# Hybrid mixer: decay rows through DRAM, fewer products for dt and group sums, three modulation blocks moved, taps and roots ordered ahead of splits

## Chip, core and metric

The kernel runs on one core of a Trainium2 chip. The metric is the device time of one execution in microseconds. The kernel before took 1097.56 us, the median of three runs (1096.56 to 1098.46).

## What is computed

The reference runs one sequence of 256 tokens with 1024 channels through two layers of three sublayers each: a feed-forward block (FFN), a mixer, and a second FFN. The mixer of the first layer is the hybrid that this change is about, that of the second layer is an mLSTM. A condition vector `c` modulates each sublayer: a product with `ada_w` gives nine blocks of shifts, scales and gates in a layer. The hybrid's core:

```python
gate_lru, x_lru, z_ssd, xbc, dt_raw = jnp.split(h @ w_in, HYB_SPLITS, axis=-1)
x_lru = causal_conv(x_lru, lru_conv_w, lru_conv_b)
y_lru = rg_lru(x_lru, ...) * jax.nn.gelu(gate_lru.astype(f32))
xbc = jax.nn.silu(causal_conv(xbc, ssd_conv_w, ssd_conv_b)).astype(f32)
dt = jax.nn.softplus(dt_raw.astype(f32) + ssd_dt_bias.astype(f32))
a = -jnp.exp(ssd_a_log.astype(f32))
y = ssd_chunked(xs, dt, a, bm, cm) + ssd_d.astype(f32)[:, None] * xs
y = y.reshape(bsz, seq, SSD_WIDTH) * jax.nn.silu(z_ssd.astype(f32))
y = rms_norm(y.reshape(bsz, seq, SSD_GROUPS, SSD_WIDTH // SSD_GROUPS), ...)
y_cat = jnp.concatenate([y_lru, y], axis=-1).astype(h.dtype)
return y_cat @ w_out
```

`ssd_chunked` cuts the tokens into two chunks of 128. For each of 16 heads it needs the running sum `acs` of `dt * a` in a chunk, and from it `decay_in = exp(acs[t] - acs[s])` for all pairs t >= s of a chunk and `decay_out = exp(acs[t])`.

## The kernel before

**Layout and stages.** Activations lie transposed: channels on the 128 partitions, the 256 tokens along the free dimension, so `x` is eight tiles of [128, 256]. All large weights lie in one stream of 128x128 tiles, in the order of use, loaded in pieces of eight tiles (512 KB) by the SP queue. The program is unrolled; six sublayers (0 to 5) follow one another. Sublayer 0 (first FFN) uses pieces 0 to 65, sublayer 1 (hybrid) pieces 66 to 119.

**Products.** Precision comes from splitting: a weight piece is cast to a high part by ScalarE (`whi`, L101) and its rest is computed by VectorE (`wlo`, L102). `multiply` (L436) issues three products for each tile: high times high, high times low, low times high. They are counted in `W.products`, three for each tile, 24 for each piece; "product n of stage s" below is that count. `h[k]` holds the high and low part of the modulated input beside each other.

**Order of work.** `Weights.next` (L123) hands out tiles; it loads and splits up to four pieces ahead (`LEAD`) into four raw buffers and six high and six low buffers. Splits are in order on each engine. `W.behind(piece, n, ins)` puts the ScalarE (n = 0) or VectorE (n = 1) half of a piece's split behind an instruction in that engine's order. `pump(i)` issues the modulation blocks that `ADA_PLAN` makes due at piece i: a DMA of 512 KB on the SP queue and one product with accumulation on VectorE (`ada`, L262), behind the last split so far. The compiler's scheduler orders the rest by its own estimate of times; every engine and the SP queue then run in that fixed order. `stand(ins, s, n)` (L312) keeps an instruction behind product n - 1 of stage s; `in_one_go` keeps a group of products together in order.

**The hybrid (L769).** `begin` computes the four B and C channels first, with the norm's sum (`rst_n1`) and spread (`rsb_n1`) put between the products. Then:
- Two and then six `xbc` channels are projected; each is convolved by one ScalarE step and three VectorE taps (`conv`, L728). They take turns in the four PSUM banks of tag `mm`, so a later projection waits for an earlier one's last tap.
- dt (L815 to L826): eight input tiles times a 128-column window whose first 16 columns are the dt weights, with three products for each tile (24 in all), copied out, transposed, and turned into dt by VectorE.
- The loop over c from 0 to 9 (L934) projects `xl` c, and from c = 2 on `z` c - 2 and the gates of the LRU. At c = 3 `decay_sums` makes `acs`. At c = 4 `decay_rows` transposes it to 16 rows and writes a high part and a rest into `stk` (rows 0 to 15 and 32 to 47).
- The loop over pairs of heads m0 = 0, 2, 4, 6 (L967): four `ab` products of a selecting column (`sel`) with `stk` put the rows of four heads on all partitions in PSUM; ScalarE makes `mt` (eight Relus with the bias `acs`, one Exp) and `ce` (two Exps), VectorE multiplies them with `cbt` and C; then 12 products give `y`. After that `xs` is updated and squared into `gacc`, and two `gl` channels (the LRU's gate) are projected.
- After m0 = 2 and m0 = 6 the group's sum `rst_g` is taken: four products over the two halves of `gacc`, which the profile shows as eight passes. Nine small VectorE steps make the reciprocal root (`rs_tokens`, `rsqrt_small`), two products spread it (`rsb_g`), and `group_norm` applies it.
- The output projection (`out_project`, L535) runs over `ys` of group 0, `ys` of group 1, and then `yl`, and traces the LRU's scans (L1057), the second `group_norm` and the gelu beside its products. It starts at product 912 of the stage; the part on group 1 starts at 1008, that on `yl` at 1104.

`mt` tiles and the `xw` tiles of `ssd_values` share two buffers (tag `mt`).

## Time and profile before

| | |
|---|---|
| median of three runs | 1097.56 us (1096.56 to 1098.46) |
| the profiled execution | 1097.25 us |
| its span, first to last instruction | 1095.5 us |
| TensorE busy | 1083.8 us, 99% |
| VectorE busy | 920.5 us, 84% |
| ScalarE busy | 639.5 us, 58% |
| mean granted TensorE clock | 0.999 |

The profile is of one execution. The page gives sums and groups; the timeline lists instructions in order of time for one engine (PE is TensorE, DVE VectorE, ACT ScalarE, SP the queue that issues DMAs), with the idle time ahead of one in brackets and what ended it. A matmul's duration there overlaps that of the next, so the time that a product costs is read from the distance of starts. Tile names stand without their numbers: `wlo` is the low part of any piece. The hybrid stage lies at about 194 to 367 us of the span.

### The profile page before, as it was taken

The page shows a single profiled execution, that of the slowest core. Times are in us where ns is not written, and L with a number is a line of the kernel's source. Part 1 is how long each engine was busy: PE and PEld are TensorE (multiplying, and loading weights), DVE is VectorE, ACT ScalarE, POOL GpSimd, SP SyncE. Part 2 cuts the span into 40 slices and gives each one's busy share as a digit, 9 for nine tenths or more (in the row PEclk, how much of TensorE's full clock was granted, in tenths as well). Part 3 has the DMA queues.
Part 4 walks back from the last instruction along what each step waited for, and adds up shares of the span by engine and source line. Part 5 has one row for each costly group of instructions (what it writes and reads, how often), then busy time and mean ns, then how long its engine had stood idle before and what let it go on. Part 6 is the DMA issues. An engine that isn't in the chain of part 4 may idle for free.

```text
span 1095.5 us, 23272 instructions
## 1 busy us (share of the span) xinstructions
PE 1083.8 (99%) x9315; PEld 1070.4 (98%) x9315; DVE 920.5 (84%) x1654; ACT 639.5 (58%) x1053; POOL 8.8 (1%) x28
## 2 busy tenths in 40 slices
PE   9999999999999999999999999999999999999997
PEld 7999999999999999999999999999999999999997
DVE  7999999899999899989698798979768868866552
ACT  5765555678986564554454455448776655544452
POOL 0000000000000000000000000010000000000000
PEclk9999999999999999999999999999999999999999
DMA  9889999556855489999848799963432664875551
GB/s 375 344 318 391 387 352 343 178 196 195 279 167 191 139 307 370 354 351 327 281 142 323 266 356 346 338 204 119 146 102 81 208 193 137 298 239 193 193 174 39
DMA packets 75534, 272.34 MB, mean 249 GB/s; under 512 B 8593, under 2 KB 9393, under 8 KB 75426
## 3 DMA queue, kind: packets, MB, share of 16 engines
q1 hardware_dynamic: 74592, 269.38, 69.7%
q8 instruction: 73, 1.20, 0.4%
q0 software_dynamic: 400, 1.04, 0.4%
q10 hardware_dynamic: 434, 0.43, 0.1%
q14 instruction: 35, 0.29, 0.1%
HBM read 269.77 MB, written 1.05 MB: 247 GB/s over the span
## 4 chain that ended last, share of the span: by engine, by line
PE 80%; DVE 12%; DMA 4%; issue 2%; ACT 1%; ACTq 0%; DVEq 0%; SPq 0%
PE gu L445 12%; PE gu L444 12%; PE gu L443 11%; PE od L445 10%; PE od L443 10%; PE od L444 10%; DVE wlo L102 4%; DMA wraw<-in_wst_dram 3%; PE zz L445 1%; PE zz L443 1%; PE zz L444 1%; DMA wgr<-in_ml_wg_dram 1%; DVE ada L262 1%; DVE xc L733 1%; PE gu_f L509 1%
## 5 line engine op out<-in xcount | busy, mean ns | idle before, releaser
L102 DVE TENSOR_TENSOR wlo<-wraw,whi 128x1024 fp32r<-128x1024 f32 x364 | 442.9, 1221 | 83.6 <-ACT whi L101 83.0
L101 ACT CAST whi<-wraw 128x1024 fp32r<-128x1024 f32 x364 | 378.2, 1050 | 210.9 <-DMA wraw<-in_wst_dram 80.2
L444 PE MATMUL gu<-hb,whi 128*128 128x256 f32 x1296 | 358.0, 276 | 0.4 <-DVE hb L668 0.3
L443 PE MATMUL gu<-hb,whi 128*128 128x256 f32 x1296 | 358.0, 276 | 0.0
L445 PE MATMUL gu<-hb,wlo 128*128 128x256 f32 x1296 | 357.9, 276 | 0.1
L444 PEld LDWEIGHTS gu<-hb,whi 128*128 128x128 f32 x1296 | 243.3, 188 | 0.8 <-DVE hb L668 0.8
L445 PEld LDWEIGHTS gu<-hb,wlo 128*128 128x128 f32 x1296 | 243.3, 188 | 0.2 <-DVE wlo L102 0.2
L443 PEld LDWEIGHTS gu<-hb,whi 128*128 128x128 f32 x1296 | 243.2, 188 | 0.0
L443 PE MATMUL od<-ph,whi 128*128 128x256 f32 x704 | 194.3, 276 | 0.0
L444 PE MATMUL od<-ph,whi 128*128 128x256 f32 x704 | 194.3, 276 | 0.0
L445 PE MATMUL od<-ph,wlo 128*128 128x256 f32 x704 | 194.3, 276 | 0.0
L262 DVE SCALAR_TENSOR_TENSOR ada<-ada,cact 128x1024 f32<-128x1024 f32 x144 | 175.3, 1218 | 1.4 <-DMA ada<-in_adaT_dram 1.3
L444 PEld LDWEIGHTS od<-ph,whi 128*128 128x128 f32 x704 | 132.1, 188 | 0.0
L445 PEld LDWEIGHTS od<-ph,wlo 128*128 128x128 f32 x704 | 132.1, 188 | 0.0
L443 PEld LDWEIGHTS od<-ph,whi 128*128 128x128 f32 x704 | 132.1, 188 | 0.0
L426 ACT CAST ph<-fg 128x256 fp32r<-128x256 f32 x88 | 35.1, 406 | 114.9 <-DVE fg L595 114.9
L427 DVE TENSOR_TENSOR ph<-fg,ph 128x256 fp32r<-128x256 f32 x88 | 36.4, 421 | 14.2 <-ACT ph L426 14.2
L416 ACT ACTIVATE sq_o<-x 128x256 f32<-128x256 f32 x42 | 17.5, 418 | 45.6 <-DVE x L571 40.6
L571 DVE SCALAR_TENSOR_TENSOR x<-od,gate,x 128x256 f32<-128x256 f32 x48 | 23.1, 481 | 24.4 <-PE od L445 24.2
L444 PE MATMUL zz<-hb,whi 128*128 128x256 f32 x128 | 36.2, 283 | 0.0
L445 PE MATMUL zz<-hb,wlo 128*128 128x256 f32 x128 | 36.1, 282 | 0.0
L443 PE MATMUL zz<-hb,whi 128*128 128x256 f32 x128 | 35.8, 279 | 0.0
(431 smaller groups left out, 1959.1 us busy)
## 6 DMA issues: line engine op xcount, KB each, us to landing
wraw<-in_wst_dram SPq DMA_DIRECT2D x366, 512.0 KB, 4.6
ada<-in_adaT_dram SPq DMA_DIRECT2D x144, 512.0 KB, 5.6
xn<-in_x_dram SPq DMA_DIRECT2D x2, 512.0 KB, 4.0
wgr<-in_ml_wg_dram POOLq DMA_DIRECT2D x3, 256.0 KB, 5.4
out_dram<-res SPq DMA_DIRECT2D x3, 128.0 KB, 2.4
out_dram<-res ACTq DMA_DIRECT2D x1, 256.0 KB
out_dram<-res SPq DMA_DIRECT2D x1, 256.0 KB, 2.9
cols<-in_cols_dram SPq DMA_DIRECT2D x1, 190.0 KB, 9.5
```

The lines of the kernel that those rows point to most:

```text
L101: raw_hi = nc.scalar.copy(hi, raw)
L102: self.last = nc.vector.tensor_tensor(out=lo, in0=raw, in1=hi.bitcast(F32), op=ALU.subtract)
L262: return nc.vector.scalar_tensor_tensor(out=raw, in0=raw, scalar=1.0, in1=cact, op0=ALU.mult, op1=ALU.mult, accum_out=mods[s][:, m:m + 1])
L416: square = nc.scalar.activation(q, x, AF.Square).ins
L426: nc.scalar.copy(hi, src)
L427: nc.vector.tensor_tensor(out=both[:, 1, :], in0=src, in1=hi.bitcast(F32), op=ALU.subtract)
L443: m = nc.tensor.matmul(dst, wh, both[:, 0, :], start=start, stop=False, skip_group_check=True)
L444: W.products += [m, nc.tensor.matmul(dst, wh, both[:, 1, :], start=False, stop=False, skip_group_check=True), nc.tensor.matmul(dst, wl, bo ...
L445: nc.tensor.matmul(dst, wl, both[:, 0, :], start=False, stop=stop, skip_group_check=True)]
L509: W.products += [nc.tensor.matmul(dst, wh, rh, start=(k == 0), stop=False), nc.tensor.matmul(dst, wh, rl, start=False, stop=False), nc.ten ...
L571: nc.vector.scalar_tensor_tensor(out=xs_t[d], in0=dst, scalar=g[:, d:d + 1], in1=xs_t[d], op0=ALU.mult, op1=ALU.add)
L733: nc.vector.scalar_tensor_tensor(out=dst[:, o:], in0=src[:, :T - o], scalar=cw(j), in1=dst[:, o:], op0=ALU.mult, op1=ALU.add)
```

## The change

1. **Decay rows.** `stk`, `sel` and the `ab` products go. ScalarE copies the 16 transposed rows to `rows`; one DMA stores them in a DRAM tile `kept`; for each pair of channel tiles one DMA loads four rows (4 KB) to every partition, straight into `mt`. Exp and Relu then read SBUF. The tiles of m0 = 0 and 2 are loaded at c = 5 and 7 and worked at c = 7 and 9 of the loop (`decay_pair`), those of m0 = 4 and 6 loaded after the squares of m0 = 0 and 2.
2. **dt.** High and low weights lie beside each other in one window, so that two products for each input tile give both sums (16 columns each), and VectorE adds them.
3. **Group sums.** VectorE folds the halves of `gacc` first; the sum takes two products in place of four.
4. **Modulation.** Blocks 40 to 42 move from the hybrid to the first FFN; blocks 16 and 17 come due at pieces 14 and 15 (17 and 18 before), 18 to 42 at pieces 17 to 42, 43 to 47 at pieces 22 to 31 of the hybrid.
5. **Order.** The low splits of four pieces go behind a tap or a root; the first two `y` groups stand at products 732 and 795; the sum of group 1 at 948 and its spread at 976; the sum and spread of `n1` are kept at 11 and 28 from both sides (`hold`); the scans go behind the second root.

```diff
-SUMS = {"n1": (1, 11), "n2": (2, 11), "n4": (4, 14)}
+SUMS = {"n1": (1, 11), "n2": (2, 11), "n4": (4, 14), "g1": (1, 948)}
+KEPT, HELD = ("n1",), 48
+SPREADS = {"n1": (1, 28), "n2": (2, 28), "g1": (1, 976)}
...
-    (0, (17, 43), range(16, 40)), (0, (43, 65), range(48, 64)), (1, (22, 37), range(40, 48)),
+    (0, (14, 16), range(16, 18)), (0, (17, 43), range(18, 43)), (0, (43, 65), range(48, 64)),
+    (1, (22, 34), range(43, 48)),
...
+    dramp = ctx.enter_context(tc.tile_pool(name="dramp", bufs=1, space=bass.MemoryType.DRAM))
...
+    def hold(ins, s, n):
+
+        holds.append((ins, 3 * PIECE * starts[s] + n))
...
+                if i == 0:
+                    W.behind(starts[1] + 9, 1, taps[-1])
...
-            wdh, wdl = (w[:, 16 * k:16 * k + P] for w in dt_parts)
-            nc.tensor.matmul(b[:, 0:T], wdh, h[k][:, 0, :], start=(k == 0), stop=False)
-            nc.tensor.matmul(b[:, 0:T], wdh, h[k][:, 1, :], start=False, stop=False)
-            nc.tensor.matmul(b[:, 0:T], wdl, h[k][:, 0, :], start=False, stop=(k == ND - 1))
+            for i in range(2):
+                nc.tensor.matmul(b[:, 0:T], dt_parts[:, 32 * k:32 * k + P], h[k][:, i, :], start=(k == i == 0),
+                                 stop=(k == ND - 1 and i == 1))
...
+        nc.vector.tensor_tensor(out=dt, in0=both[:, :, 16:32], in1=dt, op=ALU.add)
...
-            nc.vector.tensor_copy(stk[0:16, :], b[0:16, 0:T])
-            nc.vector.tensor_tensor(out=stk[32:48, :], in0=b[0:16, 0:T], in1=stk[0:16, :].bitcast(F32),
-                                    op=ALU.subtract)
+            nc.scalar.copy(rows[0:16, :], b[0:16, 0:T])
+            nc.sync.dma_start(kept, rows[0:16, :])
+
+        def decay_tile(m0):
+            mt = wk.tile([P, 2, 2, 2, P], F32, tag="mt", name=f"mt{m0}", bufs=2)
+            nc.sync.dma_start(mt.rearrange("p n i c t -> p (n i c t)"),
+                                kept.rearrange("(q h) t -> q (h t)", q=4)[m0 // 2:m0 // 2 + 1].to_broadcast([P, 4 * T]))
+            decays[m0] = mt
...
+        def decay_pair(m0):
+            g = m0 // 4
+            mt = decays.pop(m0)
+            ce = wk.tile([P, 2, 2, P], F32, tag="ce", name=f"ce{m0}", bufs=2)
+            expo = nc.scalar.activation(ce.rearrange("p n i t -> p (n i) t"),
+                                        mt.rearrange("p n i c t -> p (n i) c t")[:, :, 1, :], AF.Exp)
...
+                        nc.scalar.activation(mt[:, n, i, c, :], mt[:, n, i, c, :], AF.Relu,
+                                             bias=acs[:, c, hd:hd + 1], scale=-1.0)
+            nc.scalar.activation(mt, mt, AF.Exp, scale=-1.0)
...
+                if c == 7:
+                    W.behind(starts[1] + 31, 1, taps[-1])
...
+            if c in (5, 7):
+                decay_tile(c - 5)
+            if c in (7, 9):
+                pairs[c - 7] = decay_pair(c - 7)
...
-            ab = [ax_bank(f"ab{m}") for m in pair]
-            for m, b in zip(pair, ab):
-                for i in range(2):
-                    hd = 2 * m + i
-                    nc.tensor.matmul(b[:, i * T:(i + 1) * T], sel[:, hd:hd + 1].to_broadcast([P, P]), stk,
-                                     start=True, stop=True)
...
+            mt, ce, needed, expo = pairs.pop(m0) if m0 in pairs else decay_pair(m0)
...
+            if m0 < 4:
+                stand(products[0], 1, (732, 795)[m0 // 2])
...
+                folded = nc.vector.tensor_tensor(out=gacc[:, 0, :], in0=gacc[:, 0, :], in1=gacc[:, 1, :], op=ALU.add)
+            if m0 < 4:
+                decay_tile(m0 + 4)
...
-                roots.append(rs_tokens([gacc[:, 0, :], gacc[:, 1, :]], 512, f"g{g}", "q"))
+                roots.append(rs_tokens([gacc[:, 0, :]], 512, f"g{g}", "q"))
...
+                W.behind(starts[1] + (39, 43)[g], 1, rsqrt_ends[-1])
...
-                nc.vector.tensor_tensor_scan(out=xl[:, c, :], data0=av[:, c, :], data1=nq[:, c, :], initial=0.0,
-                                             op0=ALU.mult, op1=ALU.add)
+                with tc.issue_after(second_root.ins):
+                    nc.vector.tensor_tensor_scan(out=xl[:, c, :], data0=av[:, c, :], data1=nq[:, c, :], initial=0.0,
+                                                 op0=ALU.mult, op1=ALU.add)
...
+    for i, n in holds:
+        for m in W.products[n:n + HELD]:
+            tc.add_manual_dep(m.ins, i.ins.name, NOSYNC, reason="not later")
```

## Rows read from the trace of the kernel before

**Rows 1.** The page: the span, and busy time of the engines.

```profile
span 1095.5 us, 23272 instructions
...
PE 1083.8 (99%) x9315; PEld 1070.4 (98%) x9315; DVE 920.5 (84%) x1654; ACT 639.5 (58%) x1053; POOL 8.8 (1%) x28
```

**Rows 2.** Windows: length; busy PE, PEld, DVE, ACT, POOL; PEclk, DMA, GB/s.

```profile
45.00:60.00 15.00, 15.00 (x135) 15.00 (x134) 12.80 (x18) 12.36 (x23) 0.00 (x0) 1.00 0.73 242
...
60.00:125.00 65.00, 65.00 (x576) 65.00 (x575) 63.37 (x105) 35.77 (x57) 0.00 (x0) 1.00 0.97 367
...
245.00:285.00 40.00, 39.23 (x334) 38.07 (x334) 39.68 (x78) 33.40 (x65) 0.00 (x0) 1.00 0.66 218
```

**Rows 3.** PE timeline (start, us, what), the waits: [idle before <- what ended it].

```profile
220.79 0.36 PE L443 MATMUL xbc<-hb,whi 128*128 128x256 f32 x1 [0.28 <-DVE ssd_x L733]
...
282.85 0.28 PE L445 MATMUL ri<-xlb,wlo 128*128 128x256 f32 x1
...
283.90 0.39 PE L443 MATMUL z<-hb,whi 128*128 128x256 f32 x1 [0.77 <-DVE lru_x L733]
...
296.41 0.33 PE L1008 MATMUL y<-mt,ssd 128*64 128x128 f32 x2 [0.85 <-DVE mt L988]
...
331.61 0.68 PE L405 MATMUL rsb_g<-ident,rsy_g 128*128 128x128 f32 x4 [0.72 <-DVE rsy_g L329]
```

**Rows 4.** Timelines: piece 111's split on DVE, its first use on PE.

```profile
336.61 1.20 DVE L102 TENSOR_TENSOR wlo<-wraw,whi 128x1024 fp32r<-128x1024 f32 x1
...
342.92 0.28 PE L445 MATMUL od<-ysb,wlo 128*128 128x256 f32 x1
```

**Rows 5.** PE timeline: first `dtT` product, and the first after them.

```profile
212.08 0.28 PE L818 MATMUL dtT<-hb,wdh 128*128 128x256 f32 x1
...
214.89 0.28 PE L443 MATMUL xbc<-hb,whi 128*128 128x256 f32 x1
```

**Rows 6.** PE timeline: four `ab` products, a group's sum, and their followers.

```profile
287.45 0.63 PE L974 MATMUL ab<-stk,sel 128*128 128x256 f32 x4
...
287.92 0.28 PE L443 MATMUL gl<-hb,whi 128*128 128x256 f32 x1
...
308.06 1.03 PE L359 MATMUL rst_g<-ones,gacc 128*128 128x1 f32 x8
...
308.95 0.37 PE L444 MATMUL gl<-hb,whi 128*128 128x256 f32 x1
```

**Rows 7.** DVE timeline: a split and an ada product between `xl7`'s taps.

```profile
280.70 1.21 DVE L102 TENSOR_TENSOR wlo<-wraw,whi 128x1024 fp32r<-128x1024 f32 x1
...
282.22 1.22 DVE L262 SCALAR_TENSOR_TENSOR ada<-ada,cact 128x1024 f32<-128x1024 f32 x1
```

**Rows 8.** ACT timeline: `xl7`'s first step, four Relus, an Exp.

```profile
278.08 0.54 ACT L730 ACTIVATE lru_x<-xl,cols 128x256 f32<-128x256 f32 x1
...
292.37 1.18 ACT L983 ACTIVATE mt<-ab,acs 128x128 f32<-128x128 f32 x4
...
293.63 1.14 ACT L986 ACTIVATE mt<-mt 128x1024 f32<-128x1024 f32 x1
```

**Rows 9.** DVE timeline: first and last of the nine steps of `g1`'s root.

```profile
324.43 0.16 DVE L373 TENSOR_SCALAR rsv_g<-rst_g 128x2 f32<-128x2 f32 x1
...
331.33 0.14 DVE L329 SCALAR_TENSOR_TENSOR rsy_g<-rsw_g,rsy_g 128x2 f32<-128x2 f32 x1
```

**Rows 10.** Groups by line, 205 to 345: ada products on DVE.

```profile
L262 DVE SCALAR_TENSOR_TENSOR ada<-ada,cact 128x1024 f32<-128x1024 f32 x8 | 9.7, 1218 | 0.0
```

**Rows 11.** DVE timeline: the first of the two writes of `stk`.

```profile
260.64 0.40 DVE L864 CAST stk<-acst 16x256 fp32r<-16x256 f32 x1
```

**Rows 12.** The page's DMA issues: KB each, median us to landing.

```profile
wraw<-in_wst_dram SPq DMA_DIRECT2D x366, 512.0 KB, 4.6
...
out_dram<-res SPq DMA_DIRECT2D x3, 128.0 KB, 2.4
```

**Rows 13.** SP timeline: two loads of weights, the first to the second's end.

```profile
274.92 2.57 SPq L95 DMA_DIRECT2D wraw<-in_wst_dram  x2
```

More of the change, by code (lines that the diff above doesn't have):

```diff
@@ L364, in sum_tokens @@
                 stand(products[0], *SUMS[nm])
+                if nm in KEPT:
+                    hold(products[-1], *SUMS[nm])
         else:
@@ L406, in spread @@
                                  start=True, stop=True)
-            if nm == "n2" and b == 0:
-                stand(m, 2, 28)
+            if b == 0 and nm in SPREADS:
+                stand(m, *SPREADS[nm])
+            if b == 1 and nm in KEPT:
+                hold(m, *SPREADS[nm])
         return pb[:, 0:T]
@@ L847, in hybrid @@
         acs = acs_wide[:, 0:32].rearrange("p (c h) -> p c h", c=2)
[L848 to L849 removed]
+        rows = sp.tile([P, T], F32, name="rows")
+        kept = dramp.tile([16, T], F32, name="kept")
         dec = sp.tile([P, 16], F32, name="dec")
```

69 lines of the change are left out of this document (33 added, 36 removed).

## The prediction

> **What bounds the kernel now.** I read the page first: TensorE is busy for 1083.8 of 1095.5 us [rows 1], so little time is left in which it waits, and a change pays by taking products off TensorE or by taking away one of its few waits. Whether another engine could hold it back is read from the windows. In the stretch of the hybrid mixer from 245 to 285 us VectorE is busy for 39.68 of 40 us, ScalarE for 33.40, and DMA for 66% [rows 2]: VectorE has no idle time there, and since it works in order, whatever TensorE needs from it waits behind whatever stands ahead of it. The timeline of PE shows four such waits in this stage [rows 3]: `xbc` for a tap, `z` for a tap of `xl7`, `y0` for `mt`, and the spread of `g1` for its root. Each costs a little more than its idle time: between the starts at 282.85 and 283.90 lie 1.05 us instead of one product's 0.12 (below), so the idle 0.77 costs 0.93, 0.16 more. Splits of weights run ahead of TensorE; the smallest lead late in the stage is that of piece 111 (the 110th of the 364 splits), done at 336.61 + 1.20 = 337.81 and first used at 342.92, 5.11 us later [rows 4].
>
> **Products that go.** dt: 24 products of 256 columns take 214.89 - 212.08 = 2.81 us, 0.117 each [rows 5]; 8 go: 0.94 us. Decay rows: four `ab` products take 287.92 - 287.45 = 0.47 us before their follower starts [rows 6]; there are four such fours: 1.88 us. Group sums: the eight passes take 308.95 - 308.06 = 0.89 us [rows 6]; with one operand instead of two half of them go, in two groups: 0.89 us. All of it stands on TensorE, which has nothing else to do in that time: 3.71 us.
>
> **Waits that may go.** With 0.16 added to each idle time of [rows 3], `xbc` costs 0.44, `z` 0.93, `y0` 1.01 and the spread 0.88, together 3.26 us.
> `xbc`: two splits stand ahead of the first taps, and the edit puts the second (piece 75) behind them. It takes a full split, 1.21 us [rows 7], out of the way of a wait of 0.28: I take the wait as gone.
> `z`: a split (280.70) and an ada product (282.22) run between `xl7`'s taps, 1.2 us each [rows 7]. The edit puts the split behind the taps; the ada product may stay. TensorE comes 0.94 + 0.44 = 1.38 us earlier; VectorE is relieved of two `stk` writes before that place, about 0.8. So between nothing and about 0.6 us is left; I take 0.2, since one ada block fewer has run by then.
> `y0`: its pair of decay tiles is made inside the loop, from c = 7, instead of after it. The ACT work of a pair is eight Relus, twice 1.18, an Exp of 1.14 [rows 8] and the Exp of `ce`, some 4 us; two pairs are 8 us moved into a time in which ScalarE has 6.6 us idle [rows 2] and its casts of weights can come later. On the other side `y0` is now placed 12 products after the loop, where before it came 58 after (counted along the timeline). What is left lies between nothing and the present 1.01; I take 0.4. Relu now reads SBUF instead of PSUM, which no row of this shape prices: I set it at the four Relus' 1.18, and ScalarE's idle time covers a difference either way, and the copy of the rows, which it takes over from VectorE.
> Spread of `g1`: its root's nine steps last from 324.43 to 331.47 [rows 9], because a split, two products of 1024 columns and five scans run between them, and the scans go behind the root now. Only work of 1.2 us a piece is left to fall between. The sum stands at product 948 and the spread at 976, 28 x 0.117 = 3.3 us for the root; between nothing and all 0.88 us is left, and I take 0.4. Behind the held scans stand the output projection's last inputs, and the splits from piece 109 on; the splits of pieces 75, 97, 105 and 109 each wait for a tap or a root now, and a lead of 5.11 us at the least [rows 4] covers one split's 1.21.
> So 3.26 - 1.0 = 2.26 us is gained here.
>
> **What is added or moved.** VectorE loses three ada products, 3 x 1.22 [rows 10], and two `stk` writes of 0.40 [rows 11], 4.46 us; the folds of the two sums and a second addition of dt add an estimated 1.1, from the shapes' neighbours. The relief is 3.4 us, while TensorE comes up to 6.97 us earlier (3.71 + 3.26): the lead of piece 111 falls from 5.11 to about 1.5 us, still above zero.
> The three ada blocks go to the first FFN, two of them to 45 to 60 us, where VectorE has 15 - 12.80 = 2.20 us idle and DMA is 73% busy; the third to 60 to 125, where VectorE has 1.63 idle, but DMA is 97% busy [rows 2]. Two cost 2.44 us of VectorE there: nothing if the idle time fits, at worst all 3.66 us of the three on the path. I take nothing, since the nearest rows have 3.83 us idle for 3.66.
> The rows go out by one store of 16 KB and come back by four loads of 512 KB, all on SP's queue, where the loads of weights stand behind them; the store waits there for ScalarE's copy, each load for the store or for its tile's buffer. By the nearest rows a store takes 2.4 us to land and a load of this size 4.6 [rows 12], 7.0 together. Rows ready at about 261 [rows 11] would be back at 268, and ScalarE comes to that place of its program after `xl7`, at 278.08 [rows 8]: 10 us of slack cover it. The Trainium skill says in DMA: Bandwidth & Descriptors (Anatomy of one DMA) that a transfer counts as finished only when its last byte is confirmed in the target memory, which can take surprisingly long when that is HBM; its fit gives an estimate of 2.0 + 3.2 = 5.2 us for the pair, with the same sum. No row here shows a load that follows a store of the same bytes.
> The `n1` sum stays where it is and its spread comes one product earlier, so it could cost 0.1 us at most. The pads and the joined dt tile move no other work: nothing.
>
> **The sum.** 3.71 + 2.26 = 5.97 us off the profiled execution's 1097.25 (its span of 1095.5 and 1.75 around it): 1091.3. The median of the three runs, 1097.56, is 0.31 above it: **1091.6 us**.
>
> **Rivals.**
> *VectorE sets the pace.* It is 99% busy from 245 to 285 [rows 2]; if its order leaves TensorE's waits as they are, only the products count (3.71 us, 1093.9), and if it bounds the stage, only its relief of 3.4 (1094.2). Against it speak the lead of 5.11 us and that three of the four waits have a named piece of work in front of them that goes.
> *The first FFN pays.* If the three ada blocks don't fit beside the splits, 1.5 to 3.66 us come back: 1093.1 to 1095.3. For it speaks the 97% of DMA, against it the 27% idle just before.
> *The rows come back late (slower).* ScalarE works in order, so a decay tile that has not landed when its Exp's turn comes holds up the tanh and copies that free TensorE's banks. SP's queue is the place: a load behind weight loads that wait for a buffer goes out late, as the two at 274.92 that took 2.57 us to issue [rows 13]; behind these the first tile would land at 277.5 + 4.6 = 282.1, 4.0 us after ScalarE's turn. Four tiles that each come w late give 1091.6 + 4 w: slower than before from w = 1.5 us, and 1099.6 at w = 2. For it speaks that SP waited so in this stretch, against it the 10 us of slack. By the Trainium skill's sentence on confirmation in HBM (DMA: Bandwidth & Descriptors, Anatomy of one DMA) the store alone could bring the same w.
> *Waits moved, not removed.* The products go, but `y0`, placed 46 products earlier, waits for `mt` by what they saved: 1097.5. Against it speaks that its input starts some 10 us earlier.
>
> **How the numbers follow.** A change of 0.2%, 2.2 us, is about what a measurement of this kernel can tell from none. The forecast has a chance of 0.58, VectorE's pace 0.19, the first FFN 0.08 (0.05 of it within 0.2%), waits moved 0.06, late rows 0.09. Faster: 0.58 + 0.19 + 0.03 = 0.80; same: 0.05 + 0.06 = 0.11; slower: 0.09. At best all 6.97 us come, and the runs spread by about 1 us (1096.56 to 1098.46): 1089.6, and I go to 1089.3 for the short waits of less than 0.1 us idle that I did not price. Upwards the range takes in VectorE's pace and the first FFN, to 1095.4.
>
> **What would show it.** Right: TensorE has 32 products and passes fewer (8 + 16 + 8), no `ab` at all; the waits at `xbc` and `z` are gone or under 0.3 us; `mt0` is multiplied before the loop's last `z`; the root's nine steps take under 4 us; splits keep a lead above 1 us at pieces 109 to 113; TensorE shows no new wait from 45 to 190. Wrong: ScalarE idle before an Exp with a DMA as releaser (late rows), TensorE waiting for `wlo` in the first FFN or after piece 109, or a span that shrank by 3.7 us alone with the same four waits.

## The result: slower by 0.5%, and the profile after

| | before | after |
|---|---|---|
| median of four runs each, us | 1097.27 (1096.56 to 1098.46) | 1102.93 (1100.22 to 1105.13) |
| ratio to before, 95% interval | | 1.0050 (1.0031 to 1.0069) |
| profiled execution; its span | 1097.25; 1095.5 | 1103.5; 1101.8 |
| mean granted TensorE clock | 0.999 | 0.994 |

The forecast was 1091.6 us, so 11.3 us separate it from the result. The page shows 32 records of TensorE fewer, as the change says, and yet more busy time [rows 1]:

```profile
span 1101.8 us, 23202 instructions
...
PE 1086.5 (99%) x9283; PEld 1071.7 (97%) x9283; DVE 921.5 (84%) x1654; ACT 640.4 (58%) x1050; POOL 8.4 (1%) x26
```

Where the time went is seen when the same product of the weight stream is looked up in both traces (the first product that uses the piece's low part; start after minus start before, us):

| piece | before | after | difference | what lies between |
|---|---|---|---|---|
| 47 | 142.25 | 142.34 | +0.09 | |
| 51 | 153.13 | 153.66 | +0.53 | a split late, first FFN |
| 68 | 201.09 | 202.87 | +1.78 | the spread of `n1` waits |
| 74 | 221.10 | 221.71 | +0.61 | eight products of dt and the wait at `xbc` gone |
| 95 | 284.95 | 284.71 | -0.24 | the wait at `z` gone |
| 99 | 299.83 | 297.76 | -2.07 | `ab` products and `y0`'s wait gone |
| 115 | 353.80 | 353.43 | -0.37 | a new wait at `y4`, the lower clock behind it, small delays in the output projection |
| 121 | 371.33 | 376.04 | +4.71 | the sum of `n2`, the lower clock behind it |
| 122 | 374.65 | 380.18 | +5.53 | the rest of the lower clock |
| 233 | 678.39 | 684.50 | +6.11 | |

So the hybrid's loop gained 3.85 us from piece 68 to piece 99, about what was forecast for its products and waits. Time is lost ahead of it, in the first FFN and at `n1`, and behind it, at `y4` and above all at one place: 5.9 us at the sum of `n2`, in the first products of the next FFN, with the lower clock that follows. PE's timeline of the changed kernel shows the places (columns as in [rows 3]):

```profile
199.68 0.71 PE L415 MATMUL rsb_n<-ident,rsy_n 128*128 128x128 f32 x4 [0.82 <-DVE rsy_n L337]
...
289.15 0.66 PE L1035 MATMUL y<-mt,ssd 128*64 128x128 f32 x8
...
308.29 0.62 PE L1035 MATMUL y<-mt,ssd 128*64 128x128 f32 x6 [1.33 <-DVE mt L968]
...
329.29 0.68 PE L415 MATMUL rsb_g<-ident,rsy_g 128*128 128x128 f32 x4 [0.18 <-DVE rsy_g L337]
...
368.00 0.28 PE L522 MATMUL gu_f<-hb,whi 128*128 128x258 f32 x1
370.94 1.01 PE L367 MATMUL rst_n<-ones,sq_o 128*128 128x1 f32 x4 [2.66 <-ACT sq_o L428]
```

`y0` (289.15) has no wait left. The spread of `n1` (199.68) and `y4` (308.29) have waits that the kernel before did not have; the spread of `g1` waits 0.18 where it waited 0.72; the sum of `n2`, `rst_n`, stands 2.94 us behind the product ahead of it. What it waits for is the square of the last channel of the residual. In the kernel before, that square lay so in ACT's timeline,

```profile
368.05 0.42 ACT L416 ACTIVATE sq_o<-x 128x256 f32<-128x256 f32 x1 [1.03 <-DVE x L571]
```

and the sum so in PE's:

```profile
368.52 0.60 PE L359 MATMUL rst_n<-ones,sq_o 128*128 128x1 f32 x4
```

In the changed kernel, ACT's timeline has the square here:

```profile
370.47 0.42 ACT L428 ACTIVATE sq_o<-x 128x256 f32<-128x256 f32 x1 [1.03 <-DVE x L583]
```

Before, the square ended at 368.05 + 0.42 = 368.47 and the sum started at 368.52: no wait, but a lead of 0.05 us. After, the square ends at 370.89, 2.4 us later, and the sum follows at 370.94 by the same 0.05, while TensorE was ready at 368.12, 0.4 us earlier. So most of this wait is VectorE and ScalarE coming late, and little of it TensorE coming early. The windows of the changed kernel (columns as in [rows 2]) show what surrounds this:

```profile
60.00:125.00 65.00, 65.00 (x576) 65.00 (x575) 63.69 (x106) 35.06 (x57) 0.00 (x0) 1.00 0.97 371
125.00:190.00 65.00, 64.88 (x572) 64.68 (x571) 58.87 (x92) 31.59 (x45) 0.00 (x0) 1.00 0.95 348
285.00:308.00 23.00, 21.49 (x205) 20.46 (x204) 21.88 (x35) 23.00 (x50) 0.00 (x0) 1.00 0.65 219
308.00:328.00 20.00, 19.71 (x173) 18.76 (x174) 15.41 (x38) 13.95 (x27) 0.00 (x0) 0.91 0.46 167
370.00:380.00 10.00, 9.06 (x50) 9.06 (x51) 5.31 (x17) 2.10 (x5) 0.00 (x0) 0.66 0.24 85
```

and of the kernel before, for three stretches that [rows 2] does not have:

```profile
125.00:190.00 65.00, 65.00 (x576) 65.00 (x575) 61.12 (x98) 33.74 (x46) 0.00 (x0) 1.00 0.97 360
285.00:308.00 23.00, 22.08 (x210) 21.20 (x209) 22.95 (x37) 21.17 (x53) 0.00 (x0) 1.00 0.76 258
308.00:328.00 20.00, 19.92 (x190) 19.08 (x190) 19.02 (x39) 17.51 (x35) 0.00 (x0) 1.00 0.47 147
```

To be seen: in the first FFN DMA is as full as before, 0.97 from 60 to 125, and VectorE, with three products more to do, did less from 125 to 190 (58.87 us for 61.12): its splits come later. It is busy for 15.41 us of the 20 from 308 to 328, where it was for 19.02: 3.6 us more of idle time around the group roots. ScalarE has no idle time left from 285 to 308 (23.00 of 23.00; 21.17 before). And behind the wait at `n2` the granted clock is 0.66 over ten microseconds, that is, TensorE ran at the lower of its two levels (1.2 of 2.4 GHz) for 0.34 / 0.5 of ten, 6.8 us; from 308 to 328, behind `y4`'s wait, it is 0.91 (0.57 from 309 to 313, that is 3.4 us at the lower level).

DVE's timeline of the changed kernel has two of these late splits at the root of `n1`, one ahead of its first step and one (196.95) between its steps, and further on what answers to [rows 9] and [rows 4], the second group's root in one run and the split of piece 111:

```profile
195.34 1.22 DVE L105 TENSOR_TENSOR wlo<-wraw,whi 128x1024 fp32r<-128x1024 f32 x1
...
196.87 0.15 DVE L383 TENSOR_SCALAR rsv_n<-rst_n 128x2 f32<-128x2 f32 x1
196.95 1.22 DVE L105 TENSOR_TENSOR wlo<-wraw,whi 128x1024 fp32r<-128x1024 f32 x1
198.09 0.16 DVE L328 TENSOR_SCALAR rsy_n<-rsv_n 128x2 int32<-128x2 int32 x1
...
327.41 0.16 DVE L383 TENSOR_SCALAR rsv_g<-rst_g 128x2 f32<-128x2 f32 x1 [0.76 <-PE rst_g L367]
...
328.98 0.16 DVE L337 SCALAR_TENSOR_TENSOR rsy_g<-rsw_g,rsy_g 128x2 f32<-128x2 f32 x1
...
340.61 1.19 DVE L105 TENSOR_TENSOR wlo<-wraw,whi 128x1024 fp32r<-128x1024 f32 x1
```

and PE's timeline has the first use of that piece:

```profile
342.04 0.28 PE L457 MATMUL od<-ysb,wlo 128*128 128x256 f32 x1
```

The group root's steps take 1.7 us instead of 7.0, as ordered. Piece 111 is split 0.24 us before its use, where 1.5 was forecast and 5.11 was: TensorE came 0.9 us earlier, and the split 4.0 us later.

### The profile page after: what moved, and what is told of

Same layout as the page of the kernel before. It is cut to its first block, busy times and chain, and to the rows that moved or that the text cites. A ratio compares the mean times of both kernels' runs of the same rounds, so it can differ in the third digit from the quotient of the medians.

```text
span 1101.8 us, 23202 instructions
## 1 busy us (share of the span) xinstructions
PE 1086.5 (99%) x9283; PEld 1071.7 (97%) x9283; DVE 921.5 (84%) x1654; ACT 640.4 (58%) x1050; POOL 8.4 (1%) x26
## 4 chain that ended last, share of the span: by engine, by line
PE 68%; DVE 18%; DMA 7%; ACT 4%; issue 3%; ACTq 0%; DVEq 0%; SPq 0%
PE gu L456 10%; PE gu L457 10%; PE gu L455 10%; PE od L457 8%; PE od L456 8%; PE od L455 8%; DVE wlo L105 7%; DMA wraw<-in_wst_dram 5%; DVE ada L266 2%; ACT whi L104 2%; PE zz L457 1%; PE zz L455 1%; PE zz L456 1%; DMA wgr<-in_ml_wg_dram 1%; DVE hb L488 1%
```

## The experiments

Each run is timed against the kernel before on its own chip; the ratio is the measure, since the medians before vary from 1097.16 to 1097.64. 0.1% is 1.1 us, and what a run gains or loses in us is taken from its ratio.

**Which part loses at `n2`.**

```diff
-SUMS = {"n1": (1, 11), "n2": (2, 11), "n4": (4, 14), "g1": (1, 948)}
+SUMS = {"n1": (1, 11), "n2": (2, 35), "n4": (4, 14), "g1": (1, 948)}
...
-SPREADS = {"n1": (1, 28), "n2": (2, 28), "g1": (1, 976)}
+SPREADS = {"n1": (1, 28), "n2": (2, 52), "g1": (1, 976)}
```


> The changed kernel, with the sum of n2 placed at product 35 of stage 2 instead of 11, and its spread at 52 instead of 28. Theory (the 5.1 us that the change loses at this sum are its wait of 2.66 us for the last square of the residual, and the half clock of 6.83 us behind that wait): the sum comes 24 products, about 2.8 us, later, so its wait is under 0.5 us, the clock does not fall there, and the time is 1097 to 1099. Rival A (the residual's chain is so late that the need only moves to the next place that reads its result): a wait of 2 us or more and a half clock appear at the spread or at the first product that wants the normed rows, time 1100 to 1104. Rival B (the clock falls for another reason than the wait): no wait at the sum, but still some 6 us of half clock between 368 and 385, time 1099 to 1101.

Measured: 1097.27 us, ratio 1.0003 (0.9994 to 1.0012); no wait at the sum, granted clock 1.00 behind it. The theory holds: some 5 us hang on the place of this sum. Rival B falls: the clock of the profiled execution stays up when the wait goes, and the mean clock of the eleven runs is 0.997 to 0.999 (0.994 to 0.997 in the changed kernel).

```diff
-                W.behind(starts[1] + (39, 43)[g], 1, rsqrt_ends[-1])
...
-                with tc.issue_after(second_root.ins):
-                    nc.vector.tensor_tensor_scan(out=xl[:, c, :], data0=av[:, c, :], ...)
+                nc.vector.tensor_tensor_scan(out=xl[:, c, :], data0=av[:, c, :], ...)
```


> The changed kernel without the order around the two group roots: the splits of pieces 105 and 109 and the scans are free again to run between the root's steps. Theory (the order holds the split of piece 109, all the splits behind it and the scans back until the second root, VectorE stands idle some 4 us between 308 and 328, and the residual's chain starts 2 us late for that): the chain of residual updates starts 1.5 to 2 us earlier, the wait at the sum of n2 falls from 2.66 to under 1 us, the spread of g1 waits up to 0.7 us again, and the time is 1097 to 1099. Rival (the late decay tiles y4 and y6 make the chain late, the order does not): the wait at the sum of n2 stays above 2 us, time 1101 to 1104.

Measured: 1099.60 us, ratio 1.0021 (1.0012 to 1.0030). The wait at `n2` is gone, but for another reason than expected: the first update comes at 354.55, hardly earlier, and TensorE has lost its lead before, 1.8 us at the spread of `g1` and 1.5 at the `ysb` behind it (the output projection's input). The order buys what it was meant to; what it costs had to be asked of its two halves apart:

```diff
-                with tc.issue_after(second_root.ins):
-                    nc.vector.tensor_tensor_scan(out=xl[:, c, :], data0=av[:, c, :], ...)
+                nc.vector.tensor_tensor_scan(out=xl[:, c, :], data0=av[:, c, :], ...)
```


> The changed kernel with the eight scans free to run before the second group root; the splits of pieces 105 and 109 stay behind their roots. Theory (what is held behind the second root takes VectorE 26 us from the root's end to the first residual update, 21.8 in the kernel before, and the time in which VectorE stands idle ahead of the root is lost): scans run in that idle time, root's end to first update takes 21 to 24 us, the wait at the sum of n2 falls from 2.66 to under 1.2 us, time 1097.5 to 1101. Rival (the scans go between the root's steps instead): the spread of g1 waits over 0.7 us, the first update is no earlier than 354.5 us, time 1099.5 to 1103.

Measured: 1102.92 us, ratio 1.0049 (1.0036 to 1.0061), wait at `n2` 2.7 us, first update at 354.53. The hold of the scans decides nothing.

```diff
-                W.behind(starts[1] + (39, 43)[g], 1, rsqrt_ends[-1])
```


> The changed kernel with the splits of pieces 105 and 109 free of the group roots; the scans stay behind the second root. Theory (as for the run with the scans free: VectorE's idle time ahead of the root takes one to three splits, 1.14 us each): root's end to first residual update takes 22.5 to 25 us instead of 26, the wait at the sum of n2 falls to 0.5 to 1.8 us, time 1098 to 1102. Rival (the order of the splits decides nothing, the scans alone do): 26 us and a wait over 2.2 us stay, time 1101.5 to 1104.

Measured: 1099.18 us, ratio 1.0016 (1.0007 to 1.0025). This half does most of it. The profiled execution is the fastest of eleven (1097.13 us, mean clock 0.999; 0.996 to 0.998 in the others), so its waits may be the shortest. Its window around the roots,

```profile
308.00:328.00 20.00, 18.63 (x176) 17.58 (x176) 18.41 (x39) 16.05 (x29) 0.00 (x0) 1.00 0.53 187
```

and its PE timeline at `n2`:

```profile
367.55 0.61 PE L367 MATMUL rst_n<-ones,sq_o 128*128 128x1 f32 x4 [0.16 <-ACT sq_o L428]
```

VectorE has 18.41 us of work in the 20 around the roots again (15.41 in the changed kernel), and the sum of `n2` waits 0.16. DVE's timelines give the second root's end and the first residual update of each run:

| kernel | root's end | first update | between | wait at `n2` |
|---|---|---|---|---|
| before | 331.46 | 353.21 | 21.75 | 0 |
| changed | 329.14 | 355.07 | 25.93 | 2.66 |
| scans free | 327.96 | 354.53 | 26.57 | 2.7 |
| splits free | 329.53 | 353.00 | 23.47 | 0.16 |
| both free | 332.31 | 354.55 | 22.24 | 0 |

The first update in DVE's timeline of the changed kernel,

```profile
355.07 0.47 DVE L583 SCALAR_TENSOR_TENSOR x<-od,gate,x 128x256 f32<-128x256 f32 x1
```

and of the one with the splits free:

```profile
353.00 0.48 DVE L583 SCALAR_TENSOR_TENSOR x<-od,gate,x 128x256 f32<-128x256 f32 x1
```

Starts in two executions can differ by half a microsecond from the program's first products on (0.5 with the scans free, 0.1 or less in the other rows); the column "between" is free of that. With splits held, VectorE idles ahead of the root and has 26 us of work queued behind it; the root itself ends only 2.3 us earlier than before.

```diff
-        for j in (2, 1, 0):
+        for j in ((2, 1, 0) if n != 8 else (1, 0)):
```


> The changed kernel without the second of the four taps (j = 2) in the eight convolutions of xl; this leaves out eight operations of VectorE, 8 x 0.40 = 3.2 us, between 235 and 290 us, and nothing of TensorE. Theory (VectorE paces the stage): the residual updates begin 1.5 to 3 us earlier than at 355.1 us, the wait at the sum of n2 falls from 2.66 to under 1.2 us, time 1096.5 to 1100. Rival A (VectorE waits for TensorE and ScalarE at the two group roots anyway, so that what it saves before 290 us becomes idle time there): idle time of VectorE between 300 and 330 us grows by 2 us or more, the updates begin at 354.5 to 355.5, time 1101 to 1104.

Measured: 1103.10 us, ratio 1.0046 (1.0033 to 1.0059); updates begin at 355.04, the wait at `n2` is 2.8. My theory that VectorE's amount of work paces the stage falls. Rival A has the time and the updates right, but not the place of the idle time. The windows of the changed kernel,

```profile
235.00:300.00 65.00, 64.52 (x573) 62.62 (x572) 63.15 (x130) 57.59 (x119) 0.00 (x0) 1.00 0.67 223
300.00:330.00 30.00, 28.50 (x248) 27.18 (x248) 25.24 (x55) 23.95 (x45) 0.00 (x0) 0.94 0.52 176
```

and of this run:

```profile
235.00:300.00 65.00, 63.68 (x563) 61.86 (x564) 59.24 (x120) 56.77 (x118) 0.00 (x0) 1.00 0.66 219
300.00:330.00 30.00, 28.22 (x265) 26.86 (x261) 26.59 (x57) 24.94 (x47) 0.00 (x0) 1.00 0.54 184
```

VectorE's idle time grows from 1.85 to 5.76 us ahead of 300, where the taps were, and falls from 4.76 to 3.41 around the roots. The work that is saved turns into idle time at once, and the updates come no earlier.

```diff
-            nc.sync.dma_start(kept, rows[0:16, :])
+            nc.vector.tensor_copy(stk[0:16, :], b[0:16, 0:T])
+            nc.vector.tensor_tensor(out=stk[32:48, :], ...)
...
-            mt = decays.pop(m0)
+                    nc.tensor.matmul(b[:, i * T:(i + 1) * T], sel[:, hd:hd + 1].to_broadcast([P, P]), stk, ...)
```


> The changed kernel with the decay rows spread by products on TensorE again (two writes of the stacked rows on VectorE, four products for each pair, no store and no loads), everything else as changed. Theory (the rows through DRAM win 1.9 us of products and lose 1.3 us of wait at y4 with some 1.7 us of half clock behind it; the wait at n2 has another cause): no wait at y4 above 0.6 us and no half clock near 308, the wait at the sum of n2 stays between 1.5 and 3 us, time 1101 to 1104. Rival (the loads that come back late are what makes VectorE late afterwards): the wait at n2 goes with them, time 1095 to 1098.

Measured: 1102.73 us, ratio 1.0049 (1.0036 to 1.0062), the same as the changed kernel; the wait at `n2` is 2.6, and `y4`, which now has its own `ab`, waits 0.7. The decay rows through DRAM, together with the early work on the first two pairs, which goes with them in this run, neither cost nor gain in this order. The DMA issues of the changed kernel (columns as in [rows 12]) show what they cost themselves,

```profile
mt<-kept SPq DMA_DIRECT2D x4, 512.0 KB, 6.0
...
kept<-rows SPq DMA_DIRECT2D x1, 16.0 KB, 3.3
```

and ACT's timeline who waited:

```profile
273.64 0.63 ACT L958 ACTIVATE ce<-mt 128x512 f32<-128x512 f32 x1 [2.03 <-DMA mt<-kept]
```

The first tile was waited for by ScalarE for 2.03 us, from 271.61 on, 15 us ahead of `y0`; SP's timeline has its load go out at 267.55, behind three loads of weights that stand there from 260.66.

```diff
-KEPT, HELD = ("n1",), 48
-SPREADS = {"n1": (1, 28), "n2": (2, 28), "g1": (1, 976)}
+KEPT, HELD = (), 48
+SPREADS = {"n2": (2, 28), "g1": (1, 976)}
```


> The changed kernel with the sum of n1 and its spread free again, as in the kernel before (no placed spread at product 28, nothing held behind it). Theory (held at product 28 the spread waits 0.82 us for its root, about 1 us of PE, and this runs through to the end): the spread comes a product or more later without a wait, time 0.6 to 1.2 us less than the changed kernel. Rival (VectorE sets the time of the residual's last updates and so of the sum of n2, so what TensorE gains at n1 is lost again as a longer wait at n2): the wait at n1 is gone and that at n2 grows by 0.5 to 1 us, time within 0.4 us of the changed kernel.

Measured: 1101.32 us, ratio 1.0040 (1.0028 to 1.0052). The wait at the spread goes and one of 1.4 us at `xbc` comes; `n2` still waits 2.7. The interval overlaps that of the changed kernel: the hold is not the cause, the lateness of VectorE at `n1` is; the next run, which has the hold and not the blocks, has no wait at that spread.

**The three blocks in the first FFN.**

```diff
-    (0, (14, 16), range(16, 18)), (0, (17, 43), range(18, 43)), (0, (43, 65), range(48, 64)),
-    (1, (22, 34), range(43, 48)),
+    (0, (17, 43), range(16, 40)), (0, (43, 65), range(48, 64)), (1, (22, 37), range(40, 48)),
```


> The changed kernel with the modulation blocks where the kernel before has them (eight in the hybrid stage, none of the three in the first FFN). Theory (VectorE paces the hybrid stage: its residual updates come as late as its work says, and 3.4 us more of work there makes them later still): the first residual update comes 1 to 3 us later than at 355.1 us, the wait at the sum of n2 grows from 2.66 to 4 us or more, and the time is 1103 to 1107. Rival (the third block in the first FFN is what makes VectorE late, by splits that it pushes in between the steps of n1's root, and what leaves the stage is worth nothing): the wait of 0.4 us near 150 us and that of 0.8 us at the spread of n1 go, the wait at n2 falls below 2 us, time 1098 to 1101.

Measured: 1099.89 us, ratio 1.0022 (1.0011 to 1.0034). The theory falls again: 3.4 us more of VectorE's work in the hybrid makes it 3 us faster. The waits near 150 us and at `n1` are gone, at piece 74 TensorE is 0.8 us ahead of the kernel before, where the changed kernel is 0.6 behind it; the wait at `n2` stays at 2.2, a little above what the rival said. PE's and ACT's timelines of this run show that wait:

```profile
365.76 0.28 PE L521 MATMUL gu_f<-hb,whi 128*128 128x258 f32 x1
368.22 1.02 PE L366 MATMUL rst_n<-ones,sq_o 128*128 128x1 f32 x4 [2.17 <-ACT sq_o L427]
...
367.75 0.42 ACT L427 ACTIVATE sq_o<-x 128x256 f32<-128x256 f32 x1 [1.03 <-DVE x L582]
```

Here the square ends at 368.17, 0.3 us earlier than before the change, and TensorE is ready at 365.88, 2.6 us earlier: what it had gained is waited for.

The same lines the other way round, in the kernel before:

> The kernel before with the modulation plan of the change alone: three blocks moved from the hybrid stage to the first FFN, 3.4 us of VectorE's work and 1.5 MB of loads. Theory (the first FFN pays and the hybrid stage gains nothing, since relief of VectorE there was worth nothing in the run with fewer taps): TensorE waits 0.4 us near 150 us, splits run between the steps of n1's root and its products come about 1 us late, time 1098 to 1100. Rival (what n1 lost in the changed kernel came from its placed and held spread, and the relief counts): no new wait ahead of 210 us, time 1096 to 1097.6.

Measured: 1103.78 us, ratio 1.0062 (1.0049 to 1.0075), more than any forecast for it. PE's waits:

```profile
PE rst_n L360 <- ACT sq_o L417: 2.0, 1, 2.0
PE xbc L444 <- DVE ssd_x L734: 1.6, 1, 1.6
```

The move alone loses 6.8 us, where nothing else is changed: VectorE arrives late at the hybrid, `xbc` waits 1.6 instead of 0.28, and `n2`, which had no lead, 2.0, with a granted clock of 0.83 behind it. Which part of a block does it, load or product?

```diff
+        if i in (14, 15, 30):
+                raw = adap.tile([P, D], F32, tag="ada", name=f"extra{i}", bufs=3)
+                nc.sync.dma_start(raw, a["adaT"][40])
+                nc.vector.tensor_copy(spare[:, 0:1], raw[:, 0:1])
```

and for products only, in place of the last two lines, one product of `cact` with itself into `raw`, its sum into `spare`.

> The kernel before with three more loads of 512 KB in the first FFN, at pieces 14, 15 and 30 (a modulation block read a second time; VectorE only copies one column of each, 0.1 us), its own plan else unchanged. Theory (DMA is 97% busy there, so 1.5 MB more put all later loads of weights back, by 1.5 MB at 367 GB/s = 4.2 us at most): the raw weights of piece 65 land 3 to 5 us later than at 179.4 us, the lead of the split of piece 66 falls from 9.2 to 4 to 6.5 us, TensorE waits at the end of the first FFN or at n1, time 1098.5 to 1104. Rival (VectorE's products are what costs): leads and time as in the kernel before, 1096.8 to 1098.

> The kernel before with three more VectorE products of 1.2 us in the first FFN, at pieces 14, 15 and 30 (on a tile that is there already, the result unused), and no load. Theory (DMA is what costs): loads land as in the kernel before, the lead of the split of piece 66 stays within 1.5 us of 9.2, time 1096.8 to 1098. Rival (VectorE is the one that has no room): the lead falls by 3 us or more, time 1098.5 or more.

Measured: 1121.17 and 1120.96 us, ratios 1.021 in both. These two answer another question: they put their results into a new tile of 16 bytes for each partition, and the tiles behind it in SBUF move by it. The groups of products by line, from 165 to 185 us, of the kernel before:

```profile
L443 PE MATMUL od<-ph,whi 128*128 128x256 f32 x60 | 16.6, 276 | 0.0
```

and of the run with loads only:

```profile
L450 PE MATMUL od<-ph,whi 128*128 128x256 f32 x55 | 15.5, 282 | 0.0
...
L451 PE MATMUL od<-ph,whi 128*128 128x256 f32 x56 | 16.0, 286 | 0.0
```

Fewer products fit in the same time (167 instead of 179), in every down projection of the program. Without the new tile:

> The kernel before with three more loads of 512 KB in the first FFN, as in the run before it, but without the new tile of 16 bytes, which there moved the tiles behind it and made the products of the down projections slower (VectorE copies one column of each into a place that a later block overwrites). Theory (DMA is 97% busy there, so the loads cost): products as fast as in the kernel before, the raw weights of piece 66 land 3 to 6 us later than at 180.5 us, the lead of its split falls from 9.2 to 4 to 6.5 us, a wait appears near 150 us, time 1098 to 1104. Rival (VectorE's products are what costs): leads and time as in the kernel before, 1096.8 to 1098.

> The kernel before with three more VectorE products of 1.2 us in the first FFN, and no load, without the new tile. Theory (DMA is what costs): loads land as in the kernel before from piece 50 on, the lead of the split of piece 66 stays within 1.5 us of 9.2, time 1096.8 to 1098. Rival (VectorE is the one that has no room): the lead of piece 66 falls by 3 us or more, or TensorE waits for wlo by over 1 us, time 1098.5 or more.

Measured: loads only 1101.09 us, ratio 1.0031 (1.0019 to 1.0043); products only 1102.28, ratio 1.0037 (1.0024 to 1.0049). Both theory and rival were half right: each part costs by itself, and the tile had cost 1.7 to 1.8% beside them. The windows of the run with loads only:

```profile
60.00:125.00 65.00, 65.00 (x576) 65.00 (x575) 61.66 (x102) 35.43 (x57) 0.00 (x0) 1.00 0.99 377
125.00:190.00 65.00, 64.88 (x571) 64.68 (x570) 58.14 (x91) 31.29 (x43) 0.00 (x0) 1.00 0.93 348
```

and with products only:

```profile
60.00:125.00 65.00, 64.25 (x562) 63.88 (x561) 59.96 (x101) 31.76 (x54) 0.00 (x0) 1.00 0.91 329
125.00:190.00 65.00, 63.65 (x551) 62.88 (x551) 63.60 (x98) 34.62 (x46) 0.00 (x0) 1.00 0.99 380
```

The split of piece 66, the hybrid's first, and its first use, in the kernel before,

```profile
182.36 2.35 DVE L102 TENSOR_TENSOR wlo<-wraw,whi 128x1024 fp32r<-128x1024 f32 x2
...
193.94 0.28 PE L511 MATMUL bc<-hb,wlo 128*128 128x258 f32 x1
```

and with the loads:

```profile
189.80 1.23 DVE L102 TENSOR_TENSOR wlo<-wraw,whi 128x1024 fp32r<-128x1024 f32 x1
...
194.45 0.28 PE L517 MATMUL bc<-hb,wlo 128*128 128x258 f32 x1
```

With the loads, TensorE hardly waits in the FFN, but the split of piece 66 ends at 189.80 + 1.23 = 191.03 and is used at 194.45: a lead of 3.4 us, where it had 9.2 (ready at 184.71, used at 193.94). The changed kernel and the run with the plan alone have the same 3.4. VectorE then has splits to make among `n1`'s steps, and `xbc` waits 1.7 us. With the products, TensorE loses at once (64.25 and 63.65 us busy of 65), and the lead of piece 66 is 9.2 again afterwards. The program makes one ring of the two: a late split frees its raw buffer late, so the next load goes out late. That fits DMA's share with the products, 0.91 from 60 to 125 and 0.99 behind it (0.97 and 0.97 before); neither loads nor VectorE had room there.

**What is left when both causes go.**

`ADA_PLAN` of the kernel before, and `n2` at 35 and 52 (two of the edits above, in the changed kernel):

> The changed kernel with two things altered: the modulation blocks where the kernel before has them, and the sum of n2 at product 35 and its spread at 52 of stage 2. Theory (two separate losses: the blocks in the first FFN cost 1.5 us there and at n1 and some more behind it, the lead of zero at the sum of n2 costs its wait and the half clock behind it; without both the products and waits that the change takes away are left as gain): no wait over 1 us at the sum or the spread of n2, time 1094 to 1096, at least 1 us faster than the kernel before. Rival (the two are one loss: whatever TensorE gains, VectorE is late with the next thing): time 1096.5 to 1099, with new waits of 2 us and more in all behind 330 us.

Measured: 1096.13 us, ratio 0.9991 (0.9982 to 0.9999): the best of all, ahead of the kernel before by 1.0 us (0.1 to 2.0), and 0.1 us above what the theory said. Its one difference to the run with the blocks back is the place of `n2`'s sum and spread, and that is worth 3.4 us. In the profiled execution (1097.30 us, a slow one of the eleven) TensorE is 2.6 us ahead of before at piece 122, behind the sum and the spread, 1.8 at piece 126, and 0.1 at piece 233. PE's waits:

```profile
PE gu L456 <- DVE wlo L104: 1.2, 2, 1.0
PE od L454 <- ACT ysb L437: 1.0, 1, 1.0
...
PE gu L455 <- DVE hb L679: 0.6, 1, 0.6
```

`ADA_PLAN` of the kernel before, the splits free, and `n2` at 20 and 37:

> The changed kernel with the modulation blocks where the kernel before has them, the splits of pieces 105 and 109 free of the group roots, and the sum of n2 at product 20 and its spread at 37 of stage 2 (1 us later than now; 35 and 52 in the earlier run). Theory (each of the two causes costs its own part: with both undone, VectorE is early enough for the sum of n2 with 9 products' room, and the norm behind it is not pushed as far back as by 24): no wait over 0.5 us at n2, the waits for splits near 384 us go, time 1094 to 1096. Rival (VectorE has the same work to do between the second group root and the first product of the next FFN, so the room comes back as waits at ysb, at n2 or at gu): 1096 to 1098.5.

Measured: 1099.53 us, ratio 1.0016 (1.0007 to 1.0026). The rival holds in kind, at a time 1 us above its range: `n2` doesn't wait, but the spread of `g1` waits 1.1, the `ysb` behind it 2.1 in all, `gu` (the next FFN's products) 2.0.

`n2` at 35 and 52, and two edits more:

```diff
-    (1, (22, 34), range(43, 48)),
+    (1, (36, 47), range(43, 48)),
...
-            if m0 < 4:
-                stand(products[0], 1, (732, 795)[m0 // 2])
+            if m0 < 6:
+                stand(products[0], 1, (732, 795, 884)[m0 // 2])
```


> The changed kernel with three orders moved: the sum of n2 at product 35 and its spread at 52 of stage 2, the last five modulation blocks of the hybrid stage at pieces 36 to 46 instead of 22 to 33 (into the time in which VectorE stands idle around the group roots), and y4 placed at product 884. Theory (VectorE's idle time of some 4 us between 308 and 328 can take the five blocks, and before 308 it is relieved by 5.7 us, so that y2 and y4 no longer wait): the wait at y4 falls from 1.3 to under 0.4 us, the time is 1094 to 1096. Rival (the blocks end up beside the splits behind the second root): leads of splits at pieces 110 to 113 fall to nothing, TensorE waits there for wlo, time 1097 to 1100.

Measured: 1101.22 us, ratio 1.0034 (1.0022 to 1.0047). Neither forecast holds: `y4` no longer waits, but the group's sum waits 1.5 and the products on `ylb` in the output projection 2.9 us, and the first update comes at 357.77. The rival's waits for `wlo` are not there (0.2 us in all), and the time is above its range too.

**What a product or a VectorE operation is worth in the kernel before.**

In the kernel before, the lines of the change for dt (`dt_parts`, 16 products, the second addition) and for the group sums (the fold, one operand), and nothing else:

> The kernel before with two parts of the change alone: dt in 16 products instead of 24, and the group sums from one folded operand; nothing is placed or held, the decay rows stay on TensorE. These take 0.94 + 0.89 = 1.83 us of products away. Theory (the products are worth their time as long as VectorE is not on the path, and before it was late by little): 1095.2 to 1096.6. Rival (VectorE paces the stage, and the added folds make it slower): the waits at z, y0 and the spread of g1 grow by as much, time 1096.8 to 1098.5.

Measured: 1098.74 us, ratio 1.0013 (1.0004 to 1.0022). The theory falls: 1.83 us of products go and the time rises, to 0.2 us above the rival's range. PE's waits, to be compared with [rows 3]:

```profile
PE rsb_g L405 <- DVE rsy_g L329: 1.4, 1, 1.4
PE xbc L443 <- DVE ssd_x L733: 0.9, 1, 0.9
```

The spread of `g1` waits 1.4 (0.72 before) and `xbc` 0.9 (0.28), while `z` waits as before and `y0` less; the second root ends at 332.55, 1.1 us later than before (0.4 of it is there from the program's first products on).

The edit of the taps above, in the kernel before:

> The kernel before without the second of the four taps (j = 2) in the eight convolutions of xl; this leaves out eight operations of VectorE, 3.2 us, and none of TensorE. It asks what VectorE's work is worth where no order holds it behind a root. Theory (VectorE, 99% busy from 245 to 285 us, sets when TensorE gets z, y0 and the spread of g1, and the last square of n2 comes 0.05 us before its sum): the waits at z and y0 fall from 1.6 to under 0.6 us together, time 1094.5 to 1096.5. Rival (TensorE comes earlier to the sum of n2 and waits there by what it gained): z and y0 shrink, a wait of 0.8 us or more appears at the sum of n2, time 1096.8 to 1099.

Measured: 1097.45 us, ratio 1.0000 (0.9991 to 1.0009). `z` no longer waits, yet nothing is gained: a product of `ab` waits 0.8 us for ScalarE's `ce`, `y0` 0.5, the spread of `g1` 0.8, the sum of `n2` 0.2. The rival's wait of 0.8 us or more at `n2` is not there either.

## Why the prediction was wrong

**The step that failed most** is the one on moved work: "The relief is 3.4 us, while TensorE comes up to 6.97 us earlier ...: the lead of piece 111 falls from 5.11 to about 1.5 us, still above zero." It asked what is late next and looked only at splits. The residual's last square had a lead of 0.05 us at the sum of `n2`: unless VectorE's chain comes earlier too, what TensorE gains ahead of that is waited for there, as the run with the blocks back shows (2.6 us gained, 2.17 waited). In the changed kernel it was worse: VectorE came later, not earlier, since the splits held behind the root left it 3.6 us idle. Of the wait of 2.66 us some 2.4 is the square's lateness and 0.4 TensorE's gain; the lower clock behind it brings the loss to 5.9. Putting that sum later, or freeing the splits, takes the wait away. So in kind it was the rival *Waits moved, not removed*, at another place than the `y0` that I had named.

**The second** is "I take nothing, since the nearest rows have 3.83 us idle for 3.66" for the three blocks. This was the rival *The first FFN pays*, to which I gave 0.08; its loads alone cost 3.4 us, its products alone 4.1, the plan as a whole 6.8 in the kernel before and some 3 in the changed one, where `n2` was lost either way. The rival's price of 1.5 to 3.66 us was too low as well. Idle time of VectorE in a stretch where DMA is 97% busy was not room.

**The terms.** The 3.71 us of products did go from TensorE, but they were counted as if it had "nothing else to do in that time"; two of the three parts alone made the kernel 1.4 us slower. The waits: `xbc` and `z` went as said, `y0` went wholly (0.4 us was left to it), the spread of `g1` kept 0.18 us for 0.4. The `n1` spread, "0.1 us at most", costs 1.0: two splits, late from the FFN, stand ahead of its root's first step and behind it. A wait at `y4` was not priced; ScalarE's idle time, which was to cover the pairs, is used up from 285 to 308, and VectorE has none from 300 to 308. Which of the two makes `y4` late was not tried.

**The rival on the other side**, late rows, named the wrong wait. The store took 3.3 us and a load 6.0, 9.3 together for my 7.0. The 10 us of slack were misread: ScalarE came to the first Exp at 271.61 and not after `xl7` at 278, and the load went out only at 267.55, behind loads of weights. ScalarE waited 2.03 us for the first tile, but TensorE didn't, and products in their place gave the same time. The Trainium skill (DMA: Bandwidth & Descriptors, Anatomy of one DMA) says that completion in HBM can take surprisingly long; 3.3 us for 16 KB would fit that, but no run here shows which part of it is completion. The estimate of 5.2 us from the page's fit is 4.1 short here; the page gives that fit for DMAs that GpSimd issues, and these go out on SP's queue.

**What stays open.** Why products alone make the kernel before slower is shown as far as the later root; that it comes from the scheduler's other order of splits there is argued, not tried. The two causes, `n2` and the three blocks, explain 6.5 of the 11.3 us between forecast and result, the distance from the changed kernel to the best version. Of the 6 us forecast, that version keeps 1.0; the waits that are left are listed with it, and what took the rest was not taken apart.

## What to carry to other kernels

Before a gain on the busiest engine is counted, find the next place where it meets a chain of another engine, and read the lead there, not the wait: a wait of zero with a lead of 0.05 us can take back all of it. An order that keeps one short chain undisturbed also holds back all that is queued behind it; read that engine's idle time around the chain afterwards. Idle time of an engine in a stretch bound by loads need not be room for more loads or more work in the same ring of buffers; here it was none.

## What the hardware showed that was not expected

After a wait of 2.66 us TensorE's granted clock was at the lower level for 6.8 us, and after one of 1.33 us for 3.4 us (0.57 from 309 to 313: 0.43 / 0.5 of 4); but not in each execution. The run with `n2` later has a wait of 1.3 us at `y4` too, and its clock stayed at 1.00 from 300 to 320. The run with the rows by products has the same wait of 2.6 us, and in its profiled execution the clock stayed at 1.00 and the time was 1100.56, while others of the same kernel took up to 1104.45 at a mean clock of 0.995.

A tile of 16 bytes for each partition, put ahead of others in SBUF, lengthened the down projections' products from 276 to between 282 and 286 ns. With three loads or three products the time rose by 2.1%, and without the tile the same loads and products cost 0.31 and 0.37%.
